# Where the weights' low parts get their second operand: HBM or the raw tile's slot

## The chip, the cores and the metric

One core of one Trainium2 chip runs the program. The metric is the device time of one execution in microseconds (us), the median of several runs. TensorE is called PE in the rows, VectorE DVE, ScalarE ACT, GpSimd POOL, SyncE SP.

## What is computed

One step of a two-layer backbone (D_MODEL 2048) on 128 context tokens and 512 latent tokens, all in float32. Cut to what matters here:

```python
shift, scale, gate = split(silu(cond) @ ada_w + ada_b, 3)   # one row for context, one for latent
h = x * (1 + scale) + shift
z = h @ w_in                     # 2048 x 6656, all branches in one projection
...                              # gated recurrence, windowed attention, convolution, each gated
mix = concatenate([...])
out = mix @ w_out                # 2048 x 2048
x = layer_norm(ALPHA * x + gate * out)
```

The context tokens' keys, values and recurrence states are outputs too.

## The kernel before

Activations are 640 tokens wide: `HH` and `HL` hold them as high and low part in float32r, 16 k-tiles of 128 channels by 5 token tiles. A weight tile is 128 x 512, 256 KB in HBM, and needs the same two parts. Three products are summed per tile: high by high, high by low, low by high.

A weight tile goes through two stores. `RAW` has 8 slots (`raw0` to `raw7`), filled from HBM by SyncE: `w_load1` (L1119) for the input projection, `o_load` (L1146) for the output projection, and `ada_dve` (L346) for tiles `adawD` of the modulation's weights, which VectorE multiplies itself (L361, two halves with two instructions each, in place of TensorE). `WH` has 16 slots, 8 pairs of high and low. `split_add` makes a pair in three steps:

```python
act.copy(hi, r)                                          # L289: the high part, rounded
act.activation(lo, hi.bitcast(F32), AF.Copy, scale=-1.0) # L290: minus the high part
pool.dma_start(out=lo.bitcast(F32), in_=r, accum_op=ALU.add)  # L291: plus the raw tile
```

The last is a DMA that adds its source to its destination; GpSimd issues it, on DMA queue 0. SyncE's loads are on queue 1. 516 tiles go this way; the first tiles of a layer are split by `split` on ScalarE, VectorE and GpSimd.

`w_split` and `o_split` call it and put `r` back into `RAW` at once, in program order; the list of free slots is a queue, first in, first out. The instruction that next fills the slot waits, by semaphore, for all readers of the old content. `ahead` (L1234) splits the tiles of the next output column while TensorE works on this one and loads three tiles further. In the output projection (from L1411) `feed` splits a new tile as soon as a pair of `WH` is free and keeps up to five loads beyond that.

What else is woven in: `pump` runs steps of other generators between matrix products, among them one step of `ada_dve` per k-step in the output projection. So VectorE's queue has products of the modulation ahead of the work at a group's end: `y_gate` (L1329) multiplies a finished group by its gate and so empties its PSUM banks, `y_add` (L1335) adds it to the residual stream `Y`. A group is 512 or 256 output columns for all 5 token tiles; five of the eight banks hold it, so the next group can start on three banks and needs those that `y_gate` empties after that. The residual stream comes by `load_y` (L1300) in five transfers of 1 MB from GpSimd during the first group; in layer 1 VectorE applies the previous norm's weights to it (L1322) before the first `y_gate`.

Of the kernel before, what the change touches and what calls it, by code (L numbers as in the profile page):

```python
# [9 lines left out]
F32 = mybir.dt.float32  # L10
F32R = mybir.dt.float32r
# [3 lines left out]
ALU = mybir.AluOpType  # L15
# [109 lines left out]
def trunk(ctx: ExitStack, tc: tile.TileContext, A: dict):  # L125
    nc = tc.nc
    act, dve, pool, pe, sync = nc.scalar, nc.vector, nc.gpsimd, nc.tensor, nc.sync
# [148 lines left out]
    def pump_until(cond):  # L276
        while not cond():
            if pump(1) == 0 and not pump_ada() and not cond():
                raise RuntimeError("blocked")

    def split(hi, lo, src, lo_eng=None, hi_eng=None):
        if hi_eng:
            hi_eng.tensor_copy(hi, src)
        else:
            act.copy(hi, src)
        (lo_eng or dve).tensor_tensor(lo, src, hi.bitcast(F32), op=ALU.subtract)  # L286

    def split_add(hi, lo, r):
        act.copy(hi, r)  # L289
        act.activation(lo, hi.bitcast(F32), AF.Copy, scale=-1.0)  # L290
        pool.dma_start(out=lo.bitcast(F32), in_=r, accum_op=ALU.add)  # L291


    def adab(l, part):
# [833 lines left out]
    def w_split(l, i, c, lo_eng=None, hi_eng=None):  # L1128
        pump_until(lambda: len(WH.f) >= 2)
        hi, lo = WH.take(), WH.take()  # L1130
        r = wraw.pop((l, i, c))
        if lo_eng == "dma":
            split_add(hi, lo, r)
        else:
            split(hi, lo, r, lo_eng, hi_eng)
        wsp[l, i, c] = (hi, lo)
        RAW.put(r)
# [11 lines left out]
    def o_split(l, t):  # L1149
        pump_until(lambda: len(WH.f) >= 2)  # L1150
        hi, lo = WH.take(), WH.take()
        r = oraw.pop((l, t))
        split_add(hi, lo, r)
        osp[l, OT[t][0], OT[t][1]] = (hi, lo)
        RAW.put(r)

# [29 lines left out]
    def after0(part, n):  # L1186
        if part:
            return
        build_h0(2 * n)
        build_h0(2 * n + 1)  # L1190
        if n % 2 == 0:
            for i in range(NS):
                w_split(0, i, n // 2)
        for c in range(1, 4):
            if n == WN[c - 1]:
                for i in range(NS):
                    w_load1(0, i, c)
        if n == 7:
            w_load(0, NS)
            for c in range(4):  # L1200
                w_split(0, NS, c)
            w_load(0, NS + 1)
        if n > 0:
            start_mm(n - 1)
# [9 lines left out]
    for l in range(DEPTH):  # L1214
# [19 lines left out]
        def ahead(i, c):  # L1234
            nonlocal wnext
            m = 4 * (i + 1) + c
            if i + 1 < NN:
                w_split(l, i + 1, c, "dma")
            else:
                o_split(l, c)  # L1240
            while wnext <= m + (WLH if 0 in hold else WLA):
                if wnext < 4 * NN:
                    w_load1(l, wnext // 4, wnext % 4)
                else:
                    o_load(l, wnext - 4 * NN)
                wnext += 1
# [24 lines left out]
        def feed(deep=8):  # L1271
            nonlocal nload, nsplit
            while len(WH.f) >= 2 and nsplit < nload and deep > 0:
                o_split(l, nsplit)
                nsplit += 1
                deep -= 1
            while nload < NO and RAW.f and nload - nsplit < 5:
                o_load(l, nload)
                nload += 1
# [46 lines left out]
        def y_gate(gi, tt, b, gb):  # L1326
            w = GROUPS[gi][1]
            t = S.take()
            dve.tensor_tensor(t[:, 0:w], b[:, 0:w], gb[0 if tt == 0 else 1][:, 0:w], op=ALU.mult)  # L1329
            return t  # L1330
# [82 lines left out]
        for gi, (n0c, w) in enumerate(GROUPS[:-1]):  # L1413
# [3 lines left out]
            for k0 in range(0, KT, 2):  # L1417
                for tts, k in [(p, k) for p in ((range(3), range(3, TT)) if k0 == 0 else (range(TT),))
                               for k in (k0, k0 + 1)]:
                    hi, lo = osp[l, gi, k // kper]  # L1420
# [24 lines left out]
        w = GROUPS[gi][1]  # L1445
# [14 lines left out]
        for tt in range(TT):  # L1460
            b = banks.popleft() if last else obank[tt]
            for k in range(KT):
                hi, lo = osp[l, gi, k // 2]
# [8 lines left out]
            t = y_gate(gi, tt, b, gb)  # L1472
# [128 lines left out]
```

## Time and profile before

| | |
|---|---|
| median of 3 runs | 2306.5 us (2304.24 to 2313.06) |
| profiled execution: its own time | 2309.28 us |
| profiled execution: span of its instructions | 2307.5 us |
| mean granted clock of TensorE | 0.979 |
| TensorE matmul busy | 2192.7 us, 95% of the span |
| VectorE, ScalarE, GpSimd busy | 1395.1, 1217.7, 699.7 us |
| DMA queue 0 (from GpSimd), queue 1 (from SyncE) | 36.4% and 36.4% of 16 engines |
| read from HBM, written | 278.61 MB, 12.11 MB |

The span runs from the first to the last instruction; the execution's own time has 1.8 us around it. Busy shares are means over stages with different limits, so the prediction reads single stages: the start to 130 us, layer 0's input projection with its branches to about 930 us, its output projection to about 1150 us, then layer 1 in the same order, its output projection from 2048 us.

### The profile page before, as it was taken

To read this page: it belongs to the slowest core of one execution; us is meant where nothing else is said; L and a number is where in the kernel's file an instruction comes from. 1 tells how busy PE (TensorE), PEld (TensorE's weight loads), DVE (VectorE), ACT (ScalarE), POOL (GpSimd) and SP (SyncE) were. 2 spreads that over 40 slices of the span, in tenths; PEclk is the share of its full clock that TensorE was granted. 3 is DMA by queue.
4 is the path that set the end of the run, shared out by engine and by line. 5 is a ranking of instruction groups with operands and counts; after the bars stand their busy time and mean duration, and the time that the engine had idled before them with its cause. 6 is when DMAs were issued, how large, how long until landed. Compare 5 with 4: busy or idle time off the path is not lost.

```text
span 2307.5 us, 42648 instructions
## 1 busy us (share of the span) xinstructions
PE 2192.7 (95%) x15854; PEld 2087.2 (90%) x15854; DVE 1395.1 (60%) x3647; ACT 1217.7 (53%) x2163; POOL 699.7 (30%) x790
## 2 busy tenths in 40 slices
PE   5899999999999999979889999999999999998996
PEld 3699999999999999857789999999999999996886
DVE  3488889557679998444463666544655877123227
ACT  1177886545564435623355787764656543562332
POOL 0034334322222333312232344433222134332225
PEclk7999999999999999989999999999999999998998
DMA  9967778877767879978736676778765577688774
GB/s 370 401 173 201 197 186 199 206 194 173 182 146 180 194 188 244 273 212 201 165 127 159 158 165 162 162 182 188 164 157 127 113 173 160 151 197 228 174 167 127
DMA packets 225665, 434.06 MB, mean 188 GB/s; under 512 B 26192, under 2 KB 32048, under 8 KB 223536
## 3 DMA queue, kind: packets, MB, share of 16 engines
q0 software_dynamic: 76544, 147.38, 36.4%
q1 hardware_dynamic: 138992, 271.85, 36.4%
q10 hardware_dynamic: 9920, 12.10, 1.7%
q8 instruction: 124, 2.03, 0.4%
q14 instruction: 85, 0.70, 0.1%
HBM read 278.61 MB, written 12.11 MB: 126 GB/s over the span
## 4 chain that ended last, share of the span: by engine, by line
PE 67%; DVE 12%; DMA 8%; issue 7%; ACT 3%; POOL 2%; ACTq 0%; POOLq 0%; SPq 0%; DVEq 0%
PE z L1171 28%; PE z L1169 19%; PE m L1424 6%; DVE junk L361 6%; PE z L1424 4%; DMA x<-adaw 2%; DMA wh<-raw 2%; PE m L947 2%; PE m L861 2%; DMA s<-xT 1%; POOL wh L291 1%; PE m L915 1%; DVE s L1026 1%; DMA raw<-adawD 1%; PE z L1466 1%
## 5 line engine op out<-in xcount | busy, mean ns | idle before, releaser
L1171 PE MATMUL z<-HH,wh 128*128 128x384 f32 x3296 | 1046.8, 339 | 0.0
L1169 PE MATMUL z<-HH,wh 128*128 128x256 f32 x3296 | 926.2, 283 | 0.9 <-DVE wh L286 0.9
L291 POOL DMA_DIRECT2D wh<-raw x516 | 453.0, 910 | 1465.5 <-ACT wh L290 1335.9
L1169 PEld LDWEIGHTS z<-HH,wh 128*128 128x128 f32 x3296 | 619.8, 189 | 4.4 <-DVE wh L286 1.6
L1171 PEld LDWEIGHTS z<-HH,wh 128*128 128x128 f32 x3296 | 620.7, 188 | 1.5
L361 DVE SCALAR_TENSOR_TENSOR junk<-raw,s 128x256 bf16<-128x256 f32 x1024 | 507.8, 496 | 179.1 <-DMA raw<-adawD 148.5
L1171 PE MATMUL z<-HL,wh 128*128 128x384 f32 x1648 | 558.3, 339 | 0.0
L289 ACT CAST wh<-raw 128x512 fp32r<-128x512 f32 x516 | 316.3, 613 | 386.5 <-PE m L1424 142.4
L1169 PE MATMUL z<-HL,wh 128*128 128x256 f32 x1648 | 461.5, 280 | 0.0
L290 ACT ACTIVATE wh<-wh 128x512 fp32r<-128x512 f32 x516 | 326.3, 632 | 71.1 <-PE z L1171 56.3
L1169 PEld LDWEIGHTS z<-HL,wh 128*128 128x128 f32 x1648 | 310.9, 189 | 0.0
L1171 PEld LDWEIGHTS z<-HL,wh 128*128 128x128 f32 x1648 | 310.5, 188 | 0.0
L1026 DVE SCALAR_TENSOR_TENSOR s<-s,sm,s 128x655 f32<-128x655 f32 x240 | 224.3, 935 | 6.3
L1424 PE MATMUL m<-wh,HH 128*128 128x512 f32 (+1 forms) x768 | 207.1, 357 | 0.0
L1424 PE MATMUL z<-wh,HH 128*128 128x512 f32 (+1 forms) x512 | 155.6, 386 | 37.3 <-DVE s L1329 35.9
L1424 PEld LDWEIGHTS m<-wh,HH 128*128 128x128 f32 x768 | 137.8, 192 | 20.1
L1424 PEld LDWEIGHTS z<-wh,HH 128*128 128x128 f32 x512 | 96.8, 194 | 57.4 <-issue 35.1
L1424 PE MATMUL m<-wh,HL 128*128 128x512 f32 (+1 forms) x384 | 137.1, 357 | 3.2 <-DVE HL L286 3.2
L1424 PE MATMUL z<-wh,HL 128*128 128x512 f32 (+1 forms) x256 | 98.4, 384 | 0.0
L1095 ACT ACTIVATE s<-z 128x640 f32<-128x640 f32 x32 | 22.5, 703 | 137.7 <-PE z L1171 126.8
L1322 DVE TENSOR_TENSOR y1y<-y1y,s 128x512 f32<-128x512 f32 (+2 forms) x18 | 24.1, 1344 | 106.0 <-DMA s<-lnw_r 68.4
L1424 PEld LDWEIGHTS m<-wh,HL 128*128 128x128 f32 x384 | 73.4, 191 | 13.8 <-DVE HL L286 3.6
(554 smaller groups left out, 2656.3 us busy)
## 6 DMA issues: line engine op xcount, KB each, us to landing
wh<-raw POOLq DMA_DIRECT2D x516, 256.0 KB, 4.5
raw<-win SPq DMA_DIRECT2D x416, 256.0 KB, 3.6
raw<-adawD SPq DMA_DIRECT2D x256, 256.0 KB, 4.1
x<-adaw SPq DMA_DIRECT2D x64, 512.0 KB, 8.0
raw<-wout SPq DMA_DIRECT2D x128, 256.0 KB, 3.4
s<-crow SPq DMA_DIRECT2D x32, 256.0 KB, 5.0
s<-xT ACTq DMA_DIRECT2D x16, 320.0 KB, 7.0
s<-s ACTq DMA_DIRECT2D x80, 64.0 KB, 3.5
```

The costliest lines, as they stand in the source:

```text
L289: act.copy(hi, r)
L290: act.activation(lo, hi.bitcast(F32), AF.Copy, scale=-1.0)
L291: pool.dma_start(out=lo.bitcast(F32), in_=r, accum_op=ALU.add)
L361: dve.scalar_tensor_tensor(junk, r[:, 256 * n:256 * n + 256], 1.0, rows[0][:, 256 * c:256 * c + 256], op0=ALU.mult, op1=ALU.mult, accum_ou ...
L861: pe.matmul(b[:, 0:w], lhsT=a_, rhs=k_, start=(n_ == 0), stop=(n_ == 2))
L915: pe.transpose(b[:, o:o + 128], ps[a][:, 128 * (x + y):128 * (x + y) + 128], ident)
L947: pe.matmul(o, lhsT=v_, rhs=p_, start=(y == 0 and n_ == 0), stop=(y == len(bl) - 1 and n_ == 2))
L1026: dve.scalar_tensor_tensor(acc, u[:, t:t + AW], sm[:, cw + t:cw + t + 1], acc, op0=ALU.mult, op1=ALU.add)
L1169: pe.matmul(za, lhsT=w_, rhs=h_[:, 0:2, k, :], start=st_, stop=sp_)
L1171: pe.matmul(zb, lhsT=w_, rhs=h_[:, 2:5, k, :], start=st_, stop=sp_)
L1322: dve.tensor_tensor(yv, yv, r if gi == 0 else r.unsqueeze(1).to_broadcast([P, TT, w]), op=op)
L1424: pe.matmul(bs[tt][:, 0:w], lhsT=h_[:, tt, k, :], rhs=w_[:, o:o + w], start=(k == 0 and n_ == 0), stop=(k == KT - 1 and n_ == 2))
```

## The change

`split_add` takes the weight's address in HBM as a fourth argument, and the accumulating DMA reads it there. Both of its sides are now named float32r, before float32.

```diff
-    def split_add(hi, lo, r):
+    def split_add(hi, lo, r, w):
         act.copy(hi, r)
         act.activation(lo, hi.bitcast(F32), AF.Copy, scale=-1.0)
-        pool.dma_start(out=lo.bitcast(F32), in_=r, accum_op=ALU.add)
+        pool.dma_start(out=lo, in_=w.bitcast(F32R), accum_op=ALU.add)
...
         if lo_eng == "dma":
-            split_add(hi, lo, r)
+            split_add(hi, lo, r, A["win"][l, i, c])
...
         r = oraw.pop((l, t))
-        split_add(hi, lo, r)
+        split_add(hi, lo, r, A["wout"][l, t])
```

The order of the instructions is the same on every engine; what differs is sources and waits. SyncE in the first group of layer 0's output projection, before. In brackets are the semaphores that an instruction waits for: DMAHW are DMAs issued by SyncE or ScalarE, DMASW those issued by GpSimd, Activation is ScalarE, DVE is VectorE.

```order
L346 DMA raw0_162<-adawD 128x512 [waits DMAHW3_49,DMASW0_49,Activation_49]
L1146 DMA raw5_250<-wout 128x512 [waits DMAHW4_49,DMASW2_49,Activation_49]
L1146 DMA raw4_248<-wout 128x512 [waits DMAHW5_49,DVE_49]
L346 DMA raw2_166<-adawD 128x512 [waits DMAHW6_49,DMASW3_49,Activation_49]
L1146 DMA raw7_518<-wout 128x512 [waits DMAHW7_49,DMASW5_49,Activation_49]
L1146 DMA raw0_162<-wout 128x512 [waits DMAHW3_49,DMAHW0_49,DVE_49]
L346 DMA raw6_516<-adawD 128x512 [waits DMAHW1_49,DMASW6_49,Activation_49]
```

The same rows with the change:

```order
L346 DMA raw0_162<-adawD 128x512 [waits DMAHW3_49,Activation_49]
L1146 DMA raw5_250<-wout 128x512 [waits DMAHW4_49,Activation_49]
L1146 DMA raw4_248<-wout 128x512 [waits DMAHW5_49,DVE_49]
L346 DMA raw2_166<-adawD 128x512 [waits DMAHW6_49,Activation_49]
L1146 DMA raw7_518<-wout 128x512 [waits DMAHW7_49,Activation_49]
L1146 DMA raw0_162<-wout 128x512 [waits DMAHW3_49,DMAHW0_49,DVE_49]
L346 DMA raw6_516<-adawD 128x512 [waits DMAHW1_49,Activation_49]
```

Where a slot was last used for a weight tile, the wait for GpSimd's transfer is gone and the one for ScalarE stays; where VectorE used it last, nothing differs. GpSimd's queue at the same place, before:

```order
L291 DMA wh12_617<-raw2_166 128x512 [waits DMAHW6_49,DMASW5_49,Activation_49]
L291 DMA wh14_621<-raw6_516 128x512 [waits DMAHW7_49,DMASW6_49,Activation_49]
L291 DMA wh7_409<-raw3_246 128x512 [waits DMAHW0_49,DMASW7_49,Activation_49]
L291 DMA wh0_234<-raw0_162 128x512 [waits DMAHW1_49,DMASW0_49,Activation_49]
L1300 DMA y0y_9491<-xr 128x2048 [waits DMASW1_49,DVE_49,Pool_49]
L291 DMA wh2_238<-raw5_250 128x512 [waits DMAHW2_49,DMASW2_49,Activation_49]
```

and with the change:

```order
L291 DMA wh12_617<-wout 128x512 [waits DMASW5_49,Activation_49]
L291 DMA wh14_621<-wout 128x512 [waits DMASW6_49,Activation_49]
L291 DMA wh7_409<-wout 128x512 [waits DMASW7_49,Activation_49]
L291 DMA wh0_234<-wout 128x512 [waits DMASW0_49,Activation_49]
L1300 DMA y0y_9491<-xr 128x2048 [waits DMASW1_49,DVE_49,Pool_49]
L291 DMA wh2_238<-wout 128x512 [waits DMASW2_49,Activation_49]
```

The transfers name `wout` as source and no longer wait for the raw load (DMAHW); they wait for ScalarE as before, and for the transfer eight places earlier on GpSimd's queue (DMASW).

## Rows read from the trace of the kernel before

**Rows 1.** The page, parts 1 and 3: busy time of the engines; DMA queue 0
```profile
PE 2192.7 (95%) x15854; PEld 2087.2 (90%) x15854; DVE 1395.1 (60%) x3647; ACT 1217.7 (53%) x2163; POOL 699.7 (30%) x790
...
q0 software_dynamic: 76544, 147.38, 36.4%
```

**Rows 2.** Waits of PE, 900:1260, then 2030:2308: us in total, times, longest
```profile
PE z L1424 <- DVE s L1329: 24.5, 3, 15.3
...
PE m L1424 <- DVE HL L286: 3.2, 1, 3.2
...
PE m L1466 <- DMA wh<-raw: 0.5, 1, 0.5
...
PE z L1424 <- DVE s L1329: 11.4, 1, 11.4
```

**Rows 3.** Timeline of PE, 1129 us: start, us, instruction, [idle before]
```profile
1129.44 0.77 PE L1424 MATMUL z<-wh,HH 128*128 128x256 f32 x2 [7.24 <-DVE s L1329]
```

**Rows 4.** Waits of SyncE's queue, whole span: us in total, times, longest
```profile
SPq L1119 <- DMA wh<-raw: 1078.0, 307, 11.8
SPq L1146 <- DMA wh<-raw: 317.3, 97, 15.2
SPq L346 <- DMA wh<-raw: 188.2, 79, 11.5
```

**Rows 5.** The chain, 1110:1130: start, us, what
```profile
1117.01 3.68 DMA wh<-raw
...
1120.74 4.56 DMA raw<-adawD
```

**Rows 6.** The chain, 905:1030
```profile
925.35 4.89 DMA wh<-raw
...
930.71 4.83 DMA raw<-adawD
```

**Rows 7.** Waits of DVE, 940:1010, and its timeline at 1005 us
```profile
DVE junk L361 <- DMA raw<-adawD: 41.4, 6, 20.2
...
1005.18 2.48 DVE L1329 TENSOR_TENSOR s<-m,s 128x512 f32<-128x512 f32 x4
```

**Rows 8.** Stages, POOL's L291 alone: us, POOL busy (x count), PEclk, DMA share, GB/s
```profile
880.00:940.00 60.00, 15.27 (x17) 0.99 0.98 260
940.00:1000.00 60.00, 16.25 (x19) 0.96 1.05 289
1010.00:1120.00 110.00, 25.82 (x30) 0.98 0.81 189
2060.00:2110.00 50.00, 13.71 (x16) 0.96 1.07 306
```

**Rows 9.** DMA in 960:1000: queues (packets, MB, share of 16 engines), issues (us to landing)
```profile
q0 software_dynamic: 2427, 8.30, 74.6%
...
q1 hardware_dynamic: 2426, 4.42, 32.0%
...
wh<-raw POOLq DMA_DIRECT2D x11, 256.0 KB, 10.4
```

**Rows 10.** DMA in 1760:1790
```profile
q0 software_dynamic: 864, 1.57, 30.4%
```

**Rows 11.** DMA in 2265:2308, where queue 1 stores 20 results of 256 KB
```profile
q1 hardware_dynamic: 2880, 5.24, 34.4%
```

**Rows 12.** DMA in 2060:2110, where queue 1 carries loads of 256 KB
```profile
q1 hardware_dynamic: 3051, 5.56, 32.0%
```

**Rows 13.** Timeline of POOL, 2090 us
```profile
2090.43 0.85 POOL L291 DMA_DIRECT2D wh<-raw  x1 [2.55 <-ACT wh L290]
2090.97 0.88 POOL L1300 DMA_DIRECT2D y1y<-n  x1
```

**Rows 14.** Stages of 2 us: PE, PEld, DVE, ACT, POOL busy (x), PEclk, DMA share, GB/s
```profile
1009.00:1011.00 2.00, 2.00 (x6) 1.61 (x5) 1.97 (x6) 0.00 (x0) 0.00 (x0) 0.50 0.30 84
```

**Rows 15.** Timeline of DVE, 2103 us
```profile
2103.64 7.01 DVE L1322 TENSOR_TENSOR y1y<-y1y,s 128x512 f32<-128x512 f32 x4 [5.71 <-DMA y1y<-n]
```

## The prediction

> **What bounds the kernel now.** The page comes first. TensorE is busy for 95% of the span, and queue 0, which carries the accumulating transfers, takes 36.4% of the 16 DMA engines [rows 1]. So what the change can take away is at most the idle time of TensorE, and DMA counts only where it is late for something. The view of waits says where TensorE stands still [rows 2]: in the output projection of layer 0 it waits 24.5 us in three places for L1329, the gate multiplication that empties PSUM banks, the longest 15.3 us, and 3.2 us for L286; in layer 1 once more for L1329, 11.4 us. One of the three is 7.24 us [rows 3], which leaves 1.96 for the third. The low parts themselves are hardly ever late: the wait for a landing of `wh<-raw` in rows 2 is 0.5 us. So TensorE does not wait for the transfers that the diff touches. The question is whom they hold up.
>
> SyncE's own waits tell that [rows 4]: for the landing of an accumulating transfer, `wh<-raw`, it waits 1078.0 + 317.3 + 188.2 us before the weight loads (L1119, L1146) and the `adawD` loads (L346). A slot of `raw` can only be filled again when the accumulation out of it has landed. For most of the kernel these waits are free, since the loads run tiles ahead. They are not free where VectorE's products of the modulation (L361) wait for an `adawD` tile and the gate multiplication stands behind them on the same engine. The chain shows it twice: before 1129.4 us it is accumulation 3.68, `adawD` load 4.56, two products, L1329 [rows 5]; before 937.2 us accumulation 4.89, load 4.83, two products, L286 [rows 6].
>
> The largest stall, which ends at 1008.4 us, has the same shape: in 940 to 1010 us VectorE waits 41.4 us in six places for `adawD`, and only then reaches L1329 at 1005.18 [rows 7]. But in that stage the DMA engines are full too: their share is 0.98 in 880 to 940 us and 1.05 in 940 to 1000, against 0.81 in 1010 to 1120 [rows 8]. In 960 to 1000 both queues move the same number of packets, 2427 and 2426, one for one, and their shares add up to 106.6% [rows 9]; about 1.07 is what a full stage shows.
>
> **The change, part by part.** No instruction comes or goes and no order moves. 516 transfers take their source from HBM; `raw` is released by ScalarE's cast (L289) and no longer by the landing of the accumulation.
>
> *Price of an accumulation.* One transfer makes 144 packets (128 of 2 KB, 16 that report completion). In 1760 to 1790 us queue 0 carries only accumulations: 864 packets are 6 of them, 30.4% of 16 x 30 us is 145.9 us of engine time, 24.3 each, or 1.52 us of all 16 engines [rows 10]. A plain transfer of the same size costs 0.74 us from SBUF to HBM (34.4% of 16 x 43 us over 20 transfers [rows 11]) and 0.76 us from HBM to SBUF (32.0% of 16 x 50 us over 3051 / 144 = 21.2 [rows 12]). No row shows an accumulation out of HBM, nor one between two float32r operands, which is what both sides are now called. Its lower bound is a plain transfer, 0.74 us; its upper bound is today's price with an HBM read that overlaps nothing, 1.52 + 0.76 = 2.28 us. I take 1.52: 1.52 is twice 0.76, as if the two operands each passed the engine once, and a plain packet costs the same whichever memory it comes from. Packets that read SBUF and packets that read HBM also alternate in rows 9 without the sum of shares falling under 1.
>
> The Trainium skill (HBM Reference, Latency) gives an HBM access 0.2 us on average, which speaks against reading operands there. Paid unhidden by each of an engine's 8 data packets it would make 1.52 + 1.6 = 3.1 us, an estimate from that page, and the time would pass every figure below. The plain loads disagree: 0.76 us for 9 packets on an engine is 0.08 us a packet, so that latency is hidden there; for an accumulation no row says it. The skill (DMA: Bandwidth & Descriptors, SWDGE vs HWDGE vs iDMA) also says that a float32r destination always casts; it has no price for that, and no row here shows such a transfer.
>
> *Issue on GpSimd.* 0.85 us for an accumulation, 0.88 for the neighbouring `y1y<-n`, whose source is in HBM [rows 13]: nothing. GpSimd's queue still waits for ScalarE's negation (L290); the landing of the raw load, which it no longer needs, comes before L289 anyway.
>
> *Landing.* The accumulation may land later by some tenths of a us. What hides it is the depth of `wh`, 8 pairs: in the output projection a pair is split as soon as TensorE has freed it and used again after the other seven. Without that cover each late landing would stop TensorE by its lateness.
>
> *The raw loads.* SyncE now waits for a cast instead of a landing. In 960 to 1000 us an accumulation lands 10.4 us after its issue [rows 9], and its issue comes behind the cast, so the loads may leave some 10 us earlier, until SyncE meets its next bound: a `wout` load whose slot VectorE must first have emptied, or full DMA engines. Stage by stage, in us of TensorE's time:
>
> - Before 937.2 and before 1008.4, together: 3.2 + 15.3 of stall. What limits the gain is the DMA. The free part of the stage is (1.07 - 0.98) x 60 + (1.07 - 1.05) x 60 = 6.6 us, and some from before 880. I take 9; bounds 0 and 18.5 for the stalls alone. The granted clock also stands at 0.50, the 1.2 GHz level, in 1009 to 1011 us after the long stall [rows 14]. A shorter stall may give back the 1 us that these two lose, and some more around them; I leave it in the bound, 20.
> - Before 1068.8: 1.96 of stall, DMA not full: 2.
> - Before 1129.4: 7.24 of stall, DMA not full; the 3.68 us of the accumulation leave the chain and SyncE runs ahead besides. I take 7; bounds 3.7 and 7.2.
> - Before 2113.8: 11.4 of stall. Here VectorE waits for `y1y<-n`, issued at 2090.97 [rows 13] in a full stage (share 1.07 [rows 8]); it starts on that tile at 2103.64 and has 7.01 us of L1322 to do before L1329 [rows 15]. GpSimd issues that load when it did before; only loads moved ahead of the full stage make it land sooner. I take 2; bounds 0 and 11.4.
> - The first tiles are split on VectorE, without such transfers, and in the input projections TensorE shows no idle time behind the loads: 0.
>
> Sum: 9 + 2 + 7 + 2 = 20 us. The profiled execution takes 2309.3 us for a span of 2307.5, 2.8 us over the median of 2306.5; 2309.3 - 20 is 2289.3, which against the median is **2286.5 us**.
>
> **The rivals.**
>
> *It costs more in the full stages (slower).* If the read of HBM is not overlapped, each accumulation takes up to 0.76 us more of all engines. Between projections nothing happens: there is room. But in the full stages 17 + 19 + 16 accumulations are issued [rows 8], 52 x 0.76 = 39.5 us of DMA work that has no place, and `adawD` and `y` tiles land that much later, with L1329 behind them; the earlier loads give nothing back. The time is then 2306.5 + 39.5 = 2346. The point from which it decides: 20 us / 52 = 0.38, so a price of 1.9 us for an accumulation cancels the forecast's gain, 2.1 makes it slower. For it: no row shows this kind of transfer, neither its source nor its types. Against it: plain packets have one price for both memories. Chance 0.18.
>
> *The loads leave earlier and land no earlier.* The full stages stay full, VectorE's slots bound SyncE again, and only the two stalls outside them shrink: 2 + 4, with 3 from the rest, is 9 us, 2297.5. That is inside 0.5%, 11.5 us, about what a measurement of this kernel can tell from no change. For it: rows 8 and 9, and the program's look-ahead, which is the same. Against: rows 5, where the accumulation's 3.68 us stand in the chain by themselves. That nothing at all happens, since the wait for a cast is as late as that for a landing, belongs here. Chance 0.26.
>
> *The accumulation gets cheaper.* If what takes 1.52 us is SBUF's side, which serves both operands today, half of the reading leaves it and the price falls towards 0.74. The full stages then have room, and all five stalls go, 3.2 + 15.3 + 2.0 + 7.2 + 11.4 = 39.1 us, 2267, or a few us less if the low clock behind them goes too. Against: in rows 9 the reads of HBM by queue 1 do not run beside the accumulations, as they would if only SBUF's side were full. Chance 0.06.
>
> **How the numbers follow.** The forecast's case has 0.50: gains of 12 to 32 us, 2274 to 2295. With the cheaper accumulation that makes 0.56 for faster by over 0.5%; the second rival's 0.26 is no change; the first has 0.18 for slower. The range is 2268 to 2325: below lies the cheap accumulation, above some two thirds of the dear one (a price over 1.9 us), together 0.18.
>
> **What would show it.** SyncE's waits for `wh<-raw` should be gone, and waits of ScalarE's L289 or VectorE's L361 stand there, shorter. Queue 0 should have the same 76544 packets at about 36%, HBM reads should grow by 516 x 0.262 = 135 MB to some 414. VectorE's 41.4 us of waits for `adawD` before the first gate should halve. TensorE's waits for L1329 should read about 18 us in place of 24.5 + 11.4, and the stall before group 3 of layer 0 be close to nothing. Wrong it would be if queue 0's share rises to 45% or more (1.9 us an accumulation), if the wait for `adawD` stays although SyncE no longer waits, or if TensorE begins to wait for `wh`.

## The result and the profile after

The changed kernel takes 2289.98 us (2289.09 to 2295.02), the kernel before 2306.5 us: a ratio of 0.993 [0.9913, 0.9946], 16.5 us less. The forecast was 2286.5 us. The profiled execution of the changed kernel took 2289.98 us itself, with a span of 2288.2 us.

The page first: busy times, queue 0 (packets, MB, share of 16 engines) and HBM.

```profile
PE 2185.4 (96%) x15854; PEld 2080.8 (91%) x15854; DVE 1393.0 (61%) x3647; ACT 1216.5 (53%) x2163; POOL 700.6 (31%) x790
...
q0 software_dynamic: 76544, 147.38, 37.7%
...
HBM read 413.87 MB, written 12.11 MB: 186 GB/s over the span
```

The change does what it says: 76544 packets as before [rows 1], read now from HBM, 413.87 MB in place of 278.61. In the median the low parts' transfers land 5.5 us (`wh<-win`) and 5.7 us (`wh<-wout`) after their issue, before 4.5. The span is 19.3 us shorter; that is more than the 16.5 us between the medians, since the profiled execution before lay 2.8 us over its median. TensorE's idle time, span less busy time, fell from 2307.5 - 2192.7 = 114.8 to 2288.2 - 2185.4 = 102.8 us: 12.0 us. The other 7.3 us are busy time of the same 15854 matmuls. That is the granted clock, whose mean rose from 0.979 to 0.987, and the stages of 2 us show where. (About a third of that rise lies in the first 130 us, 0.88 to 0.93, where TensorE's busy time did not fall: 97.5 and 97.8 us.) First the kernel before, right behind its stalls at 525, 937, 1129 and 2113 us (length, PE, PEld, DVE, ACT, POOL busy, PEclk, DMA share, GB/s):

```profile
526.00:528.00 2.00, 2.00 (x9) 2.00 (x9) 1.36 (x4) 1.97 (x5) 0.00 (x0) 0.50 0.61 114
939.00:941.00 2.00, 2.00 (x6) 1.51 (x6) 2.00 (x4) 1.97 (x4) 0.83 (x1) 0.50 0.86 202
1131.00:1133.00 2.00, 2.00 (x12) 2.00 (x11) 1.93 (x5) 0.00 (x0) 0.00 (x0) 0.50 0.28 48
2115.00:2117.00 2.00, 2.00 (x6) 1.52 (x6) 1.97 (x5) 0.00 (x0) 0.00 (x0) 0.50 0.04 8
```

The same places in the changed kernel:

```profile
527.00:529.00 2.00, 2.00 (x15) 2.00 (x15) 1.90 (x12) 1.40 (x4) 0.27 (x1) 1.00 0.94 217
938.00:940.00 2.00, 2.00 (x10) 1.65 (x10) 1.95 (x3) 2.00 (x5) 0.56 (x1) 1.00 0.95 249
1110.00:1112.00 2.00, 2.00 (x19) 2.00 (x18) 1.97 (x5) 0.00 (x0) 0.00 (x0) 1.00 0.68 65
2096.00:2098.00 2.00, 2.00 (x6) 1.52 (x6) 1.93 (x5) 0.00 (x0) 0.00 (x0) 0.50 0.03 8
```

PEclk 0.50 is the 1.2 GHz level: TensorE is busy all of the two microseconds and does little more than half of the matmuls (12 against 19 in the third stage). Behind the stalls of 3.2, 3.2 and 7.2 us, which the change removed or cut, it runs at the full level now; behind the long one of layer 1 nothing differs in this slice. PE's busy time times one minus PEclk, summed over the slices behind the stalls at 525, 937, 1008, 1129 and 2113 us, is 10.7 us before and 4.7 after: some 6 of the 7.3 us. Behind the stall of 1.96 us the clock stayed at 1.00.

SyncE's waits over the whole span (us in total, times, longest) show the new releasers. The 1609 us that its loads waited for the landing of `wh<-raw` (1583.5 in [rows 4], 25.3 more before L1452) are gone; ScalarE's cast (L289) and VectorE's products (L361) release the slots, as predicted. The new waits were also to be shorter, and that they hardly are: all waits of these loads for a slot, smaller rows included, come to some 1640 us, before to some 1710. The length of SyncE's waits is not what changed.

```profile
SPq L1119 <- ACT wh L289: 685.5, 223, 15.0
SPq L346 <- DVE junk L361: 369.0, 143, 7.1
SPq L1146 <- ACT wh L289: 254.8, 89, 21.0
SPq L346 <- ACT wh L289: 137.4, 52, 8.3
```

TensorE's waits in layer 0's output projection, then in layer 1's:

```profile
PE z L1424 <- DVE s L1329: 15.0, 2, 13.3
...
PE m L1466 <- DMA wh<-wout: 1.8, 2, 1.2
...
PE z L1424 <- DVE s L1329: 13.4, 1, 13.4
```

And the three gates by TensorE's timeline (start, us, instruction, idle before):

```profile
996.16 1.19 PE L1424 MATMUL z<-wh,HH 128*128 128x512 f32 x2 [13.30 <-DVE s L1329]
...
1108.99 0.47 PE L1424 MATMUL z<-wh,HH 128*128 128x256 f32 x2 [1.67 <-DVE s L1329]
...
2094.73 1.19 PE L1424 MATMUL z<-wh,HH 128*128 128x512 f32 x2 [13.39 <-DVE s L1329]
```

Against [rows 2, 3]: the wait for L286 and the 1.96 us wait are gone, the 7.24 us one is 1.67. But the largest is 13.30 after 15.3 us, and layer 1's grew from 11.4 to 13.4. The lead over the kernel before is 1008.40 - 996.16 = 12.2 us at the first gate, 1129.44 - 1108.99 = 20.5 us at the third, and 19.1 us at layer 1's gate. So everything was won in layer 0, and the two long stalls are the two that the change did not remove. Grown on TensorE are the waits for the low part itself, 1.8 us here and before 0.5 [rows 2].

Each of these stalls is read from one execution. How far two executions can differ is seen from the first experiment below, which takes the time of the kernel before and waits as it does: its stalls at the same gates are 17.8, 2.2, 6.9 and 11.5 us, where the kernel before has 15.3, 2.0, 7.2 and 11.4. So the third gate's fall is clear; the 2 us less at the first gate are not, since the types alone make 2.4 us of difference there.

The lead begins well before these gates. The same matrix product of the input projection starts at 539.62 us before and at 534.35 after: 5.3 us were won at the stall at 525 us. The chain of the kernel before that ends there with TensorE's L861 (start, us, what; its first part):

```profile
481.17 6.39 DMA wh<-raw
487.62 3.05 DMA raw<-win
490.77 0.63 ACT wh L289
```

An accumulation holds the slot, the raw load leaves late, and ScalarE's cast of it (L289) comes late. ScalarE takes its work in order, so the attention's exponentials (L879) come late behind the cast, and over VectorE's L876 that reaches TensorE. ScalarE's waits for `raw<-win` over the whole span were 57.8 us in 31 places; with the change they are 13.6 us in 8.

### The profile page after: what moved, and what is told of

Read it like the earlier page. It is cut to its first block, busy times and chain, and to the rows that moved or that the text cites. A ratio compares the mean times of both kernels' runs of the same rounds, so it can differ in the third digit from the quotient of the medians.

```text
span 2288.2 us, 42327 instructions
## 1 busy us (share of the span) xinstructions
PE 2185.4 (96%) x15854; PEld 2080.8 (91%) x15854; DVE 1393.0 (61%) x3647; ACT 1216.5 (53%) x2163; POOL 700.6 (31%) x790
## 3 DMA queue, kind: packets, MB, share of 16 engines
q0 software_dynamic: 76544, 147.38, 37.7%
HBM read 413.87 MB, written 12.11 MB: 186 GB/s over the span
## 5 line engine op out<-in xcount | busy, mean ns | idle before, releaser
L291 POOL DMA_DIRECT2D wh<-win x388 | 344.7, 934 | 1098.5 <-ACT wh L290 1017.0
L361 DVE SCALAR_TENSOR_TENSOR junk<-raw,s 128x256 bf16<-128x256 f32 x1024 | 502.5, 491 | 140.1 <-DMA raw<-adawD 111.9
L289 ACT CAST wh<-raw 128x512 fp32r<-128x512 f32 x516 | 316.1, 613 | 326.7 <-PE m L1424 131.1
L290 ACT ACTIVATE wh<-wh 128x512 fp32r<-128x512 f32 x516 | 326.4, 632 | 84.2 <-PE z L1171 69.5
L1026 DVE SCALAR_TENSOR_TENSOR s<-s,sm,s 128x655 f32<-128x655 f32 x240 | 229.0, 954 | 6.3
L291 POOL DMA_DIRECT2D wh<-wout x128 | 110.3, 862 | 347.1 <-ACT wh L290 336.2
L1424 PE MATMUL z<-wh,HH 128*128 128x512 f32 (+1 forms) x512 | 154.5, 384 | 29.8 <-DVE s L1329 28.4
L361 DVE DVE_READ_ACCUMULATOR junk<-raw,s 128x1 f32 x1024 | 83.5, 82 | 0.0
```

The lines of the kernel that those rows point to most:

```text
L291: pool.dma_start(out=lo, in_=w.bitcast(F32R), accum_op=ALU.add)
L361: dve.scalar_tensor_tensor(junk, r[:, 256 * n:256 * n + 256], 1.0, rows[0][:, 256 * c:256 * c + 256], op0=ALU.mult, op1=ALU.mult, accum_ou ...
L1026: dve.scalar_tensor_tensor(acc, u[:, t:t + AW], sm[:, cw + t:cw + t + 1], acc, op0=ALU.mult, op1=ALU.add)
L1424: pe.matmul(bs[tt][:, 0:w], lhsT=h_[:, tt, k, :], rhs=w_[:, o:o + w], start=(k == 0 and n_ == 0), stop=(k == KT - 1 and n_ == 2))
```

## The experiments

Theory: the time was lost because a slot of `raw` stayed taken until the accumulation out of it had landed. Rivals: the float32r types or another price of the transfer; and, for the two long stalls, that only the full DMA engines hold them. Each time stands beside runs of the kernel before on the same chip, and the ratio is to those.

**The types alone.** The kernel before, with the new types on its old source:

```diff
-        pool.dma_start(out=lo.bitcast(F32), in_=r, accum_op=ALU.add)
+        pool.dma_start(out=lo, in_=r.bitcast(F32R), accum_op=ALU.add)
```

> Source back in the raw slot, both sides named float32r: the types of the change alone. If the gain comes from SyncE no longer waiting for the accumulation's landing (the theory), this is the kernel before: 2306 us within 4, SyncE's waits for wh<-raw near 1600 us in all, stalls before L1329 near 15, 2, 7 and 11 us. If the types matter (the rival), 2295 or less, or a price of an accumulation other than 1.52 us.

Measured: 2307.11 us, ratio 0.9997 [0.9987, 1.0006]. Queue 0 (36.5%) and SyncE's first wait are those of before:

```profile
SPq L1119 <- DMA wh<-raw: 1083.0, 304, 12.6
```

The types cost nothing and give nothing. What is left is the source, and with it the release of the slot. The reverse, HBM as source with float32 types, was not tried.

**The price of the source.** No kernel of its own, but the DMA view of both traces in 1740 to 1770 us, where queue 0 carries only accumulations; before, then after (packets, MB, share of 16 engines):

```profile
q0 software_dynamic: 947, 1.71, 33.5%
```

```profile
q0 software_dynamic: 898, 1.64, 38.5%
```

33.5% of 16 x 30 us over 947 / 144 accumulations is 24.4 us of engine time each, 1.53 us of 16 engines; 38.5% over 898 / 144 is 29.6 us, 1.85 us. In this window the price came near the 1.9 us at which the prediction saw the gain cancelled. It is among the dearest: the same sum over 1250 to 2040 us, where the input projection of layer 1 runs and there is room, gives 1.57 us before (39.0%, 28318 packets) and 1.60 after (40.0%, 28460). Over the whole run it hardly rose: 37.7% of 2288.2 against 36.4% of 2307.5 us is 23 us more for 516 transfers, 0.04 us each, 3%. Where the engines are full it did not rise at all. In [rows 9] queue 0 moved 2427 packets and 8.30 MB in 40 us with a share of 74.6%; the changed kernel in the same place of the program, 945 to 985 us:

```profile
q0 software_dynamic: 2417, 8.31, 72.9%
```

So it is a little dearer where there is room, and what TensorE lost by that is at most its waits for the low part itself, 3.1 us in the whole run after 0.5. In the packet records the median 2 KB packet of queue 0 takes 178 ns in both kernels; the share over 400 ns grew from 0.15% to 3.4%. These are the first packets of a transfer. In 1250 to 2040 us of the changed kernel 89 accumulations stand at least 0.5 us apart from the next; of their 574 packets over 400 ns, 461 are among the first 32 of the 128 and one among the last 48. The first 16 take 318 ns in the mean and the last 16 take 179. Before, it was 184 and 206.

**The slot held again, with HBM as source.** A small transfer behind each accumulation reads one column of `r`, on GpSimd's queue, so that the slot has to wait for a landing there again. The control issues the same transfer, out of `ident`, and holds nothing.

```diff
+    dm = new("dm", [P, 16])
+    dmn = deque(range(16))
...
+        dmn.rotate(1)
+        pool.dma_start(out=dm[:, dmn[0]:dmn[0] + 1], in_=r[:, 0:1])
```

(in the control `in_=ident[:, 0:1]`)

> Source in HBM, and behind each accumulation GpSimd issues a 4-byte-per-partition read of the raw slot into a spare tile, so the slot is held about as long as before. Theory: SyncE waits again for GpSimd's transfers, over 1200 us in all, the five stalls come back to some 39 us in sum, and the time is 10 to 22 us over that of e4_free, which issues the same small transfers. Rival (the source in HBM is itself the gain): the same as e4_free within 4 us.

> The control of e3_hold: the small transfers read a constant tile instead of the raw slot, so the slot is free at the cast as in the changed kernel. Both theories: the changed kernel's 2290 us plus what 516 small transfers cost, 0 to 10 us, SyncE's waits as in the changed kernel.

Measured: held 2358.07 us, ratio 1.0225 [1.0198, 1.0252]; control 2321.08 us, 1.0061 [1.0038, 1.0084]. SyncE's first wait and TensorE's wait for the gate, held:

```profile
SPq L1123 <- DMA dm<-raw: 1118.7, 304, 10.5
...
PE z L1428 <- DVE s L1333: 42.2, 4, 15.8
```

and in the control:

```profile
SPq L1123 <- ACT wh L291: 711.3, 229, 15.3
...
PE z L1428 <- DVE s L1333: 27.6, 2, 16.5
...
PE m L543 <- DVE s L537: 18.6, 14, 1.7
```

The sign is the theory's: held, SyncE waits as before the change, and TensorE's four stalls at the gates are back, although the source is HBM in both. Both sizes were missed. Holding costs 37 us over the control, more than the change gave, so it does more than undo the change: the small transfer is issued behind the accumulation on GpSimd and lands 4.8 us after its own issue (the accumulation 5.0), so later still. And the control costs 31 us where 0 to 10 were expected. A new wait shows in its last row: 18.6 us in front of L543, where the kernels before and after the change have 5.5 and 5.1 (L539 there), and the stall before the attention's products is back, 3.5 us, although the slot is free. GpSimd's busy time grew by 300 us for 516 issues; that its queue holds up the recurrence's small steps is likely, but was not isolated. So this pair shows that holding the slot costs time; how much the change gains from the release it does not show.

**Each projection alone.** The source from HBM in `o_split` only, with the raw tile as fourth argument in `w_split`, and the other way round:

```diff
-            split_add(hi, lo, r, A["win"][l, i, c])
+            split_add(hi, lo, r, r)
```

```diff
-        split_add(hi, lo, r, A["wout"][l, t])
+        split_add(hi, lo, r, r)
```

> Only the output projection's accumulations read HBM; those of the input projection read their slot as before. Theory (each wait taken away pays where it stood): the stalls of 2.0 and 7.2 us before the second and fourth group of layer 0 shrink as in the changed kernel, to under 2 us, those before L861 and the first group (3.2 and 3.2 us) stay, the gain is 6 to 11 us of the changed kernel's 17. Rival (the lead is won in the input projection and only carried along): gain under 3 us.

> The other half: only the input projection's accumulations read HBM. Theory: the stalls before L861 and the first group go, with the clock behind them, those of 2.0 and 7.2 us stay, the gain is 5 to 10 us, and the two halves add up to the changed kernel's 17 within 4. Rival: the gain is over 14 us here and the output projection's part is nothing.

Measured: output projection alone 2297.48 us, ratio 0.9957 [0.9941, 0.9972]; input projection alone 2303.74 us, 0.9976 [0.9967, 0.9985]. The product of the two is 0.993, the whole change. TensorE's timeline, output projection alone:

```profile
936.46 0.50 PE L1424 MATMUL m<-wh,HL 128*128 128x512 f32 x1 [2.30 <-DVE HL L286]
...
1003.29 1.19 PE L1424 MATMUL z<-wh,HH 128*128 128x512 f32 x2 [12.61 <-DVE s L1329]
...
1116.98 0.77 PE L1424 MATMUL z<-wh,HH 128*128 128x256 f32 x2 [2.56 <-DVE s L1329]
```

and input projection alone:

```profile
1000.14 1.19 PE L1424 MATMUL z<-wh,HH 128*128 128x512 f32 x2 [17.44 <-DVE s L1329]
...
1121.71 0.77 PE L1424 MATMUL z<-wh,HH 128*128 128x256 f32 x2 [7.71 <-DVE s L1329]
```

In medians that is 11.0 us, at the upper end of what was expected, and 4.8 us, just under it. The halves part. The output projection's transfers are what shortens the third gate, 7.24 to 2.56 us (under 2 was expected). The input projection's take away the two short stalls ahead of that stage, at 525 and at 937 us; with the slot held there, those stay (at 525 us, 3.8 us in the first of the two kernels). ScalarE's waits for `raw<-win` go with them: 62.8 us in the first kernel, 13.1 in the second. In the second TensorE then comes to the first gate early and waits there 17.44 us, about as long as the kernel with the types alone (17.8): part of the lead is given back at the next full stage.

**The full stage relieved.** 12 tiles of each layer's first output group are split with GpSimd's subtraction in place of the accumulating transfer, which takes 12 x 1.5 = 18 us of all DMA engines out of the stage. The edit does two more things: ScalarE's negation (L290) falls away for these tiles, and their slots stay taken until GpSimd's subtraction.

```diff
-        split_add(hi, lo, r, A["wout"][l, t])
+        if OT[t][0] == 0 and t >= 4:
+            split(hi, lo, r, pool)
+        else:
+            split_add(hi, lo, r, A["wout"][l, t])
```

> The changed kernel, but in the first group of each output projection tiles 4 to 15 get their low part by a subtraction on GpSimd (L286, about 1.3 us) and not by an accumulating transfer. Theory (full DMA engines are what is left of the two long stalls): 12 x 1.52 = 18 us of DMA work leave each of the two full stages, the stalls of 13.3 and 13.4 us fall under 5 each, the time to 2262 to 2275 us. Rival (the stalls are set by the order of issue, GpSimd's y loads behind its queue and SyncE behind VectorE): stalls over 10 us each, time 2284 to 2294.

Measured: 2279.86 us, ratio 0.9879 [0.9864, 0.9894]. The first gates of both layers:

```profile
991.17 1.19 PE L1427 MATMUL z<-wh,HH 128*128 128x512 f32 x2 [7.73 <-DVE s L1332]
...
2084.91 1.19 PE L1427 MATMUL z<-wh,HH 128*128 128x512 f32 x2 [8.60 <-DVE s L1332]
```

Both fell by 5 us, not to under 5: between theory and rival. The full DMA is a part of these stalls, as far as this edit isolates it, and not all of them. The edit has a price as well: while GpSimd subtracts, VectorE's own subtraction of a 128 x 640 tile (L286) takes 1.91 us at 940.8 us, in the changed kernel 0.83.

**And the residual stream a step earlier.** On top of that, `load_y` is called at `k0` 0, 2, 4, 6, 8 and no longer at 2 to 10:

```diff
-                if gi == 0 and k0 in (2, 4, 6, 8, 10):
-                    load_y(k0 // 2 - 1)
+                if gi == 0 and k0 in (0, 2, 4, 6, 8):
+                    load_y(k0 // 2)
```

> e6_pool12 with the five y loads one step (two k-tiles, 6.8 us) earlier. Theory (the stall in layer 1 is the last y tile's landing plus 7 us of L1322): the stall before L1329 in layer 1 falls from 8.6 us to under 3, that in layer 0, which hangs on adawD, stays within 2 us of 7.7; time 2268 to 2275 us. Rival (full DMA engines alone decide): both within 2 us of e6_pool12, time 2277 to 2283.

Measured: 2271.09 us, ratio 0.9833 [0.9813, 0.9853]. Layer 1's first stall fell from 8.60 to 3.20 us, close to what was expected, so the landing of its `y` tiles was the longer part of it. Layer 0's fell to 4.53, which was a miss: it was expected to stay at 7.7.

**And fewer modulation tiles ahead of the first gate.** On top of both, the steps of `ada_dve` are pumped at 0.6 per k-step in the first group and at 1.2 in the others, in place of 1.0 throughout; their number is the same.

```diff
-                        pump(1, RWO)
+                        pump(1, (0.6, 1.2, 1.2, 1.2)[gi])
```

> e9_pool12_yearly, with the modulation's products at 0.6 steps per k-tile in the first group of the output projection and 1.2 in the next ones. Theory (layer 0's stall is VectorE waiting for adawD tiles that share full DMA engines): that stall falls under 2 us too, time 2258 to 2268 us, unless the products that are put off are late for the last group, which waits for all of them. Rival: the stall only moves, time within 4 us of e9_pool12_yearly.

Measured: 2267.06 us, ratio 0.982 [0.9801, 0.9838]. Waits in layer 0's output projection:

```profile
PE z L1427 <- DVE s L1332: 2.7, 2, 1.8
```

In layer 1 the stall at the gate is 1.4 us, for a split of ScalarE. The two long stalls are gone; the repetition below has 3.5 us in layer 1. The 4 us over the kernel before this one are not certain by themselves: the ranges overlap.

**The change once more, on relieved stages.** The last kernel with the raw tile as source, and itself again on the same chip:

```diff
-        pool.dma_start(out=lo, in_=w.bitcast(F32R), accum_op=ALU.add)
+        pool.dma_start(out=lo, in_=r.bitcast(F32R), accum_op=ALU.add)
```

> e10_adaslow with the accumulations reading the raw slot again, so the change undone where the full stages have been relieved. Theory (the slot's wait costs wherever VectorE's queue hangs on a load, full engines or not): it is 8 to 18 us slower than e10_adaslow, with SyncE waiting over 1200 us for wh<-raw. Rival (with room on the DMA engines the loads land in time either way): within 4 us of e10_adaslow's 2267.

> e10_adaslow once more on the same chip, for the comparison with e11_adaslow_slot: 2262 to 2271 us.

Measured: slot 2286.66 us, ratio 0.9908 [0.989, 0.9925]; HBM 2268.55 us, 0.9827 [0.9808, 0.9846]. The source is worth 18.1 us here, just over what was expected. With the slot: SyncE's first wait, VectorE's for `adawD` over the whole span, and TensorE at the first and third gate:

```profile
SPq L1119 <- DMA wh<-raw: 1060.3, 306, 13.4
...
DVE junk L361 <- DMA raw<-adawD: 122.5, 40, 10.6
...
995.46 1.19 PE L1427 MATMUL z<-wh,HH 128*128 128x512 f32 x2 [5.44 <-DVE s L1332]
...
1115.86 0.77 PE L1427 MATMUL z<-wh,HH 128*128 128x256 f32 x2 [7.20 <-DVE s L1332]
```

With HBM:

```profile
SPq L1119 <- ACT wh L289: 732.2, 237, 14.6
...
DVE junk L361 <- DMA raw<-adawD: 89.4, 26, 8.4
...
PE z L1427 <- DVE s L1332: 5.7, 2, 3.5
```

One name in one line differs, and the chain of the theory moves as a whole: SyncE's wait for the landing, VectorE's wait for `adawD` (122.5 to 89.4 us), the gate behind it (7.2 us at the third gate; the sum over the whole span is 14.7 us with the slot, 5.7 with HBM). The stall at 525 us is there with the slot, 3.6 us, and not with HBM, and ScalarE's waits for `raw<-win` fall from 54.1 to 11.6 us. So the size of the gain holds without the long stalls. This pair changes the source and the release together; that it is the release, the held pair shows, in sign. It is also the fastest version here, some 22 us under the changed kernel by the two runs of it.

## Why the prediction held, and where it didn't

*Mechanism: right, but not at the gate with the largest term.* The new releasers of SyncE's waits, queue 0's 37.7% (about 36 forecast), 414 MB of HBM reads and the third gate read as forecast, and the held pair shows that a slot taken until a landing costs time. But TensorE's waits for L1329 are 28.4 us where about 18 were forecast, and one of the signs of being wrong came: ahead of the first gate the wait for `adawD` stayed, although SyncE no longer waits for landings. The issue on GpSimd cost nothing: 934 and 862 ns in place of 910.

*Price: right in the sum.* 1.52 us was taken, 3% more was measured over the run. The first rival's 1.9 us was nearly reached in a window of 30 us with room and not in the full stage. Late landings were taken to be covered; TensorE's waits for `wh`, another sign of being wrong, grew by 2.6 us.

*The sum: right by two errors against each other.* Forecast were 20 us; measured are 16.5 between the medians, 19.3 between the profiled executions. That these lie so close is luck. All 20 were priced as idle time of TensorE, of which 12.0 went; 7.3 us came from the clock. The step that failed was "I leave it in the bound": [rows 14] showed slow matmuls behind the long stall, and the term that belonged behind it and behind the others was set to zero. By the slices it was 1.6 to 2.9 us behind each of the five stalls of 3.2 us and more.

*Before 937.2 and 1008.4, 9 us forecast, 12.2 us of lead found, from other places.* The sentence "in the input projections TensorE shows no idle time behind the loads: 0" failed: at 525 us TensorE waited 3.2 us for L876 on VectorE, behind ScalarE and a late load, and that went with the input projection's part of the change, 5.3 us with the clock. The two stalls that were priced gave the other 6.9 of the 12.2 us: 4.9 at 937 us, with the clock (the same matrix product starts at 947.81 us before and at 937.59 after), and 2.0 at the large stall, no more than two executions differ by. Here the second rival was right for its place. VectorE's waits for `adawD` ahead of that gate, after the change:

```profile
DVE junk L361 <- DMA raw<-adawD: 37.3, 6, 12.1
...
964.83 0.42 DVE L361 SCALAR_TENSOR_TENSOR junk<-raw,s 128x256 bf16<-128x256 f32 x1 [5.28 <-DMA raw<-adawD]
...
971.91 0.42 DVE L361 SCALAR_TENSOR_TENSOR junk<-raw,s 128x256 bf16<-128x256 f32 x1 [5.25 <-DMA raw<-adawD]
...
992.94 2.48 DVE L1329 TENSOR_TENSOR s<-m,s 128x512 f32<-128x512 f32 x4
```

The same place before:

```profile
981.00 0.42 DVE L361 SCALAR_TENSOR_TENSOR junk<-raw,s 128x256 bf16<-128x256 f32 x1 [5.20 <-DMA raw<-adawD]
...
988.10 0.43 DVE L361 SCALAR_TENSOR_TENSOR junk<-raw,s 128x256 bf16<-128x256 f32 x1 [5.27 <-DMA raw<-adawD]
```

41.4 us [rows 7] became 37.3 and not the half. The first of the six waits fell from 20.2 to 12.1 us. After it a tile comes every 7.1 us with either source (981.00 and 988.10 before, 964.83 and 971.91 after), whoever releases its slot. The median `adawD` load lands 10.4 us after its issue in 960 to 1000 us before, and 11.8 us in 945 to 985 after: loads that left earlier took longer. What held this stall was the full stage and the number of `adawD` tiles in it, as far as the three relieving edits show, which removed it together; the first, which takes 12 accumulations away, took 5.6 of 13.3 us.

*Third gate, 7 forecast:* 7.24 to 1.67, 5.6 us, and the clock behind it. *Second gate, 2:* 1.96, all gone.

*Layer 1, 2 us forecast: the stall grew by 2 us.* "Only loads moved ahead of the full stage make it land sooner" was the condition, and no load moved far enough. GpSimd's issue of the last `y` load, VectorE's start on it, and the landings in 2042 to 2092 us, after the change:

```profile
2069.89 0.88 POOL L1300 DMA_DIRECT2D y1y<-n  x1
...
2084.58 7.01 DVE L1322 TENSOR_TENSOR y1y<-y1y,s 128x512 f32<-128x512 f32 x4 [6.14 <-DMA y1y<-n]
...
y1y<-n POOLq DMA_DIRECT2D x5, 1024.0 KB, 13.6
...
raw<-wout SPq DMA_DIRECT2D x13, 256.0 KB, 10.1
```

The landings before, in 2060 to 2110 us:

```profile
y1y<-n POOLq DMA_DIRECT2D x5, 1024.0 KB, 12.3
raw<-wout SPq DMA_DIRECT2D x17, 256.0 KB, 8.8
```

From issue to use it is 14.7 us, before 12.7 [rows 13, 15]. The raw loads that SyncE may now send earlier stand in the same full engines, and every transfer there lands later: `raw<-wout` 10.1 us in place of 8.8, `y1y<-n` 13.6 in place of 12.3. Harm by the earlier release is likely here, and small: with the slot in the output projection this stall is 11.4, 11.5 and 12.0 us in three kernels, with HBM 12.3 and 13.4, and on the relieved stages 0.9 with the slot, 3.5 and none with HBM. That the landing of the `y` tiles sets the stall is supported by moving their loads a step forward, which takes 5 of its 8.6 us; that the raw loads are what delays them was not tried by itself.

## What to carry to other kernels

In this program a transfer's source stays taken until it lands, so where buffers are what is short, reading an operand again from HBM can be cheaper than holding it; look who waits for the slot, not who waits for the transfer, and follow a late load through every engine that takes it in order. An earlier release paid here where the next load could still land in time: at 525 us, at 937 us as a full stage began, at the third gate. At the two long gates, deep in full stages, it paid nothing that is sure, and there a transfer less, or work spread over later groups, helped. Price a stall of TensorE with the slow stretch behind it.

## What was not expected of the hardware

An accumulation out of HBM took 1.60 us of 16 engines in a stage with room (1.57 out of SBUF), up to 1.85 in one window of it; the excess lies in the first packets of a transfer. In a full stage queue 0 took no more than before. Behind a stall as short as 3.2 us the granted clock was 0.50 for 2 us and more, a loss about half as long as the stall. 516 transfers of 4 bytes per partition, 0.87 us each in the median to issue on GpSimd, cost 31 us in a kernel in which GpSimd is busy 31% of the span. And VectorE's subtraction out of SBUF took more than twice as long, 1.91 in place of 0.83 us, beside one on GpSimd.
